# The beginning of a trunk kernel: plain float32 products for the first two weight pieces, and the second k-tile's adaLN weights loaded earlier

## The chip, the cores and the metric

The kernel runs on one core of a Trainium2 chip. TensorE (PE) multiplies, VectorE (DVE) and ScalarE (ACT) do elementwise work, SyncE (SP) issues the loads, and each of them works through its own list of instructions in order. The metric is device microseconds of one execution; less is better. Times inside an execution are counted from the start of the span that the profiler recorded.

## The reference

A decoder trunk with two layers, width 2048, 256 positions, all in float32. The part that matters here is the first layer's input side: a modulation computed from the vector `c`, applied to `x`, and then multiplied with a large weight.

```python
def _adaln(c, w, b):
    mod = jax.nn.silu(c) @ w + b
    shift, scale, gate = jnp.split(mod, 3, axis=-1)
...
h = x * (1.0 + scale) + shift
...
proj = h @ in_w                     # (256, 2048) @ (2048, 10304)
z, xBC, dt = jnp.split(proj, [SSD_D_INNER, SSD_D_INNER + SSD_CONV_DIM], axis=-1)
```

After that come a causal convolution, a chunked state-space scan, an output product, layer norm, shared keys and values, and an attention layer. None of these is touched.

## The kernel before

**h, one k-tile at a time.** The 2048 features of `h` are 16 k-tiles of 128, numbered 0 to 15 here. For each k-tile two 128x2048 arrays of adaLN weights are loaded (`araw`, 1024 KB each, first scale and then shift). DVE multiplies each with silu(c) and sums it along the row (line L279, "a dot" below), then adds the bias (L284, writes `mod`). ACT makes the modulated tile `htmp` out of `xt` and `mod` (L445) and rounds it to a float32r copy, the high part `hhi` (L446); DVE subtracts that from `htmp` and so has the low part `hlo` (L447). Both parts are in the tile that the profile calls `actT`. `xt` is loaded for two k-tiles at once. One call of `h_step` is one dot, and the shift's call also starts the steps behind it.

**Weights, one piece at a time.** A piece is a 128x1024 array (`raw`, 512 KB): two k-tiles by 512 output columns. ACT rounds it to `whi` (L99), DVE makes `wlo` (L101), and PE multiplies three times: whi by hhi, whi by hlo, wlo by hhi. In `cm_piece` (L144 to L146) the weights stand still and 256 positions stream, so that a piece has 24 products, 12 for each k-tile. In `tm_piece` (L198 to L200) `h` stands still and 512 columns stream, with 12 products in a piece. There are 6 buffers for `raw`, 4 for `whi` and 4 for `wlo`; `araw` has 4.

**The order of the beginning.** While `h` is still being made, PE already multiplies those pieces whose k-tiles exist. A table in the program (`order`) lists 58 pieces, 0 to 57. Pieces 0 to 6 need k-tiles 0 and 1 alone, piece 7 is the first that needs k-tiles 2 and 3, and pieces whose accumulation is left off are copied out of PSUM by ACT (`put_away`, L520). Each pass of the loop over `order` fetches a later piece, splits up to two, multiplies one, and calls `h_step` as often as the ratio 4/7 asks. The order in which the instructions then stand on each engine is set by the framework's scheduler when the program is built, by its priorities and by explicit `issue_after` constraints.

**Loads.** All go through SP's list in order. At most eight are outstanding: the ninth waits for the first to land, and so on. A load into a buffer that is still read waits for its reader, and everything behind it on SP's list waits too.

Of the kernel before, what the change touches and what calls it, by code (L numbers as in the profile page):

```python
# [49 lines left out]
def trunk(ctx, tc, xT, x, c, par, cst, bias, lnrow, ada, wdt, win, wxs, wout, wk, wv, wbin, wbout, out):  # L50
# [45 lines left out]
    def split(raw, into=None, after=None):  # L96

        hi, lo = into or [wp.tile([P, 1024], F32R, name=n, bufs=4) for n in ("whi", "wlo")]
        copied.append(S.activation(hi, raw, AF.Copy))  # L99
        with tc.issue_after(after) if after is not None else ExitStack():  # L100
            latest.append(V.tensor_tensor(lo, raw, hi.bitcast(F32), op=ALU.subtract))  # L101
        return hi.rearrange("p (k n) -> p k n", k=2), lo.rearrange("p (k n) -> p k n", k=2)
# [28 lines left out]

    state = [0]

    def cm_piece(src, q, ps, ahi, alo, k0=0, k1=KT, w=None, after=None):


        hi, lo = w or split(load_piece(src[q]), after=after)
        for k in range(2):
            kt = 2 * q + k
            for n in range(4):  # L140
                o = ps[n // 2][:, n % 2, :]
                c_ = slice(n * P, n * P + P)
                first = kt == k0 and n % 2 == 0
                T.matmul(o, hi[:, k, c_], ahi[:, kt, :], start=first, stop=False, skip_group_check=True)  # L144
                T.matmul(o, hi[:, k, c_], alo[:, kt, :], start=False, stop=False, skip_group_check=True)  # L145
                T.matmul(o, lo[:, k, c_], ahi[:, kt, :], start=False, stop=kt == k1 - 1, skip_group_check=True)  # L146

    def acc_pair(pool=None):
        return [(pool or mm).tile([P, 2, L], F32, name="acc") for _ in range(2)]
# [131 lines left out]

    def ada_bias(layer, kts, kinds):
        m = mod[layer][:, kts, kinds]
        V.tensor_tensor(m, m, adab[:, layer, kts, kinds], op=ALU.add)  # L284

    def gate_out(layer):

# [30 lines left out]
    with ExitStack() as cA:  # L318
# [15 lines left out]
        with ExitStack() as cS:  # L334
# [78 lines left out]
            with ExitStack() as c0:  # L413
# [4 lines left out]
                raws, xts, late = [], {}, []  # L418
# [10 lines left out]
                def h_step():  # L429

                    _, kind, kt = cols[h_step.i]
                    raw = raws[h_step.i]
                    h_step.i += 1
                    if kind == "scale" and kt % 2 == 0 and kt:
                        fetch_x(kt)
                    ada_dot(0, kind, kt, raw)
                    if kt > 1:
                        pin[0] = None
                    fetch()
                    while late:  # L440
                        late.pop()()
                    if kind == "shift":
                        ada_bias(0, slice(kt, kt + 1), slice(0, 2))
                        t = pe.tile([P, L], F32, name="htmp")
                        S.activation(t, xts[kt // 2][:, kt % 2, :], AF.Identity, bias=shift(0, kt), scale=scale(0, kt))  # L445
                        S.activation(hhi[:, kt, :], t, AF.Copy)  # L446
# [24 lines left out]
                def fetch_piece():  # L471
                    if len(pieces) < len(order):
                        k, q, _ = order[len(pieces)]
                        pieces.append(load_piece(source[k][q]))

                fetch()
                fetch()
                fetch_x(0)
                nc.sync.dma_start(adab_, par[:, :NB])
                V.tensor_scalar(adab[:, :, :, 1:3], adab[:, :, :, 1:3], 1.0, None, op0=ALU.add)  # L480
                fetch_piece()
                fetch_piece()
                fetch()
                fetch_piece()
                for _ in range(2):
                    for _ in range(2):
                        h_step()
                    while late:
                        pin[0] = late.pop()().ins
                    fetch_piece()  # L490

                def dt_piece(q, raw):

# [25 lines left out]
                            else:  # L519
                                S.activation(place, ps[w], AF.Copy)  # L520

                begin, done, ended, halves = {}, set(), [], {}
                for i, (k, q, ends) in enumerate(order):
                    fetch_piece()
                    if i == 16:
# [677 lines left out]
```

## Time and profile before

| | |
|---|---|
| median of 3 runs | 1247.58 us (1247.24 to 1248.12) |
| the profiled execution | 1247.47 us |
| its span in the profile | 1245.7 us |
| PE busy | 1216.8 us, 98% |
| DVE busy | 1029.4 us, 83% |
| ACT busy | 702.5 us, 56% |
| loads, first five of 40 slices | 381, 422, 421, 422, 421 GB/s |

A slice is 31 us. In the first five slices, which are the part in which `h` is made, the loads run at one constant rate; later they have room. A row of the timeline gives start, duration, engine, line, operation, what is written and read, and, in brackets, how long the engine sat idle before and what released it. A row of the windows gives the stretch, its length and the busy time of each engine, then the clock that PE was granted (1.00 is full), the share of DMA time and the rate.

### The profile page before, as it was taken

The page shows a single profiled execution, that of the slowest core. Times are in us where ns is not written, and L with a number is a line of the kernel's source. Part 1 is how long each engine was busy: PE and PEld are TensorE (multiplying, and loading weights), DVE is VectorE, ACT ScalarE, POOL GpSimd, SP SyncE. Part 2 cuts the span into 40 slices and gives each one's busy share as a digit, 9 for nine tenths or more (in the row PEclk, how much of TensorE's full clock was granted, in tenths as well). Part 3 has the DMA queues.
Part 4 walks back from the last instruction along what each step waited for, and adds up shares of the span by engine and source line. Part 5 has one row for each costly group of instructions (what it writes and reads, how often), then busy time and mean ns, then how long its engine had stood idle before and what let it go on. Part 6 is the DMA issues. An engine that isn't in the chain of part 4 may idle for free.

```text
span 1245.7 us, 18736 instructions
## 1 busy us (share of the span) xinstructions
PE 1216.8 (98%) x7086; PEld 1043.1 (84%) x7086; DVE 1029.4 (83%) x1454; ACT 702.5 (56%) x1045; POOL 0.2 (0%) x4
## 2 busy tenths in 40 slices
PE   4999999999999999999999999999999999999997
PEld 4989998898888888888888788888888888888886
DVE  6999986999987989899768678879888867658777
ACT  3645477868597789654335554443445644445631
POOL 0000000000000000000000000000000000000000
PEclk9999999999999999999999999999999999999999
DMA  9999977687556456699998569988998774463751
GB/s 381 422 421 422 421 266 252 223 287 263 211 186 220 155 183 194 227 334 351 337 333 288 187 213 375 363 329 344 354 382 314 238 242 135 136 204 117 232 175 67
DMA packets 80586, 335.88 MB, mean 270 GB/s; under 512 B 9104, under 2 KB 9328, under 8 KB 67696
## 3 DMA queue, kind: packets, MB, share of 16 engines
q1 hardware_dynamic: 80496, 334.69, 74.6%
q8 instruction: 55, 0.90, 0.3%
q14 instruction: 35, 0.29, 0.1%
HBM read 332.47 MB, written 2.18 MB: 269 GB/s over the span
## 4 chain that ended last, share of the span: by engine, by line
PE 86%; DVE 6%; DMA 4%; ACT 2%; issue 2%; SPq 0%; DVEq 0%; ACTq 0%
PE acc L173 21%; PE acc L199 12%; PE acc L200 12%; PE acc L198 12%; PE acc L176 11%; PE acc L144 3%; PE acc L146 3%; PE acc L145 3%; DMA araw<-in_ada 2%; DVE araw L279 2%; DVE wlo L101 2%; PE py L657 1%; ACT whi L99 1%; PE acc L866 1%; PE aux L969 1%
## 5 line engine op out<-in xcount | busy, mean ns | idle before, releaser
L99 ACT ACTIVATE whi<-raw 128x1024 fp32r<-128x1024 f32 x392 | 411.2, 1058 | 369.9 <-PE acc L200 135.9
L101 DVE TENSOR_TENSOR wlo<-raw,whi 128x1024 fp32r<-128x1024 f32 x392 | 472.7, 1220 | 135.9 <-ACT whi L99 128.5
L173 PE MATMUL acc<-actT,whi 128*128 128x512 f32 x1280 | 405.3, 397 | 0.0
L176 PEld LDWEIGHTS acc<-actT,wlo 128*128 128x128 f32 x1280 | 239.1, 188 | 59.1 <-DVE wlo L101 4.3
L199 PE MATMUL acc<-wlo,actT 128*128 128x512 f32 x656 | 257.5, 393 | 0.6 <-DVE wlo L101 0.5
L176 PE MATMUL acc<-actT,wlo 128*128 128x256 f32 x1280 | 253.4, 279 | 1.7 <-DVE wlo L101 1.2
L198 PE MATMUL acc<-whi,actT 128*128 128x512 f32 x656 | 253.1, 394 | 0.0
L279 DVE SCALAR_TENSOR_TENSOR araw<-araw,cb__72 128x2048 f32<-128x2048 f32 x96 | 219.3, 2285 | 12.1 <-DMA araw<-in_ada 11.8
L173 PEld LDWEIGHTS acc<-actT,whi 128*128 128x128 f32 x1280 | 195.9, 189 | 0.4
L200 PE MATMUL acc<-whi,actT 128*128 128x512 f32 x432 | 168.9, 391 | 0.0
L199 PEld LDWEIGHTS acc<-wlo,actT 128*128 128x128 f32 x656 | 123.2, 188 | 28.0 <-DVE wlo L101 3.1
L198 PEld LDWEIGHTS acc<-whi,actT 128*128 128x128 f32 x656 | 122.5, 188 | 24.2
L144 PE MATMUL acc<-actT,whi 128*128 128x256 f32 x384 | 109.1, 288 | 17.6 <-ACT actT L446 17.4
L145 PE MATMUL acc<-actT,whi 128*128 128x256 f32 x384 | 109.4, 287 | 0.0
L146 PE MATMUL acc<-actT,wlo 128*128 128x256 f32 x384 | 107.5, 287 | 0.9 <-DVE wlo L101 0.9
L200 PEld LDWEIGHTS acc<-whi,actT 128*128 128x128 f32 x432 | 81.1, 188 | 16.6
L144 PEld LDWEIGHTS acc<-actT,whi 128*128 128x128 f32 x384 | 74.5, 195 | 18.6 <-ACT actT L446 17.6
L200 PE MATMUL acc<-whi,ylo 128*128 128x512 f32 x224 | 87.6, 391 | 0.0
L145 PEld LDWEIGHTS acc<-actT,whi 128*128 128x128 f32 x384 | 75.1, 196 | 0.3
L146 PEld LDWEIGHTS acc<-actT,wlo 128*128 128x128 f32 x384 | 73.9, 196 | 1.3 <-DVE wlo L101 1.3
L200 PEld LDWEIGHTS acc<-whi,ylo 128*128 128x128 f32 x224 | 42.1, 188 | 8.5
L615 ACT ACTIVATE seg<-cbc,cumT 128x128 f32<-128x128 f32 x128 | 41.0, 389 | 4.9 <-DVE wlo L101 2.3
(273 smaller groups left out, 1108.8 us busy)
## 6 DMA issues: line engine op xcount, KB each, us to landing
araw<-in_ada SPq DMA_DIRECT2D x96, 1024.0 KB, 7.5
raw<-in_win SPq DMA_DIRECT2D x112, 512.0 KB, 6.8
raw<-in_wout SPq DMA_DIRECT2D x64, 512.0 KB, 5.8
raw<-in_wbin SPq DMA_DIRECT2D x64, 512.0 KB, 3.7
raw<-in_wxs SPq DMA_DIRECT2D x48, 512.0 KB, 4.6
raw<-in_wv SPq DMA_DIRECT2D x48, 512.0 KB, 6.7
raw<-in_wk SPq DMA_DIRECT2D x48, 512.0 KB, 7.1
cbc<-cumd SPq DMA_DIRECT2D x16, 512.0 KB, 4.7
```

Source lines behind the costliest of these rows:

```text
L99: copied.append(S.activation(hi, raw, AF.Copy))
L101: latest.append(V.tensor_tensor(lo, raw, hi.bitcast(F32), op=ALU.subtract))
L144: T.matmul(o, hi[:, k, c_], ahi[:, kt, :], start=first, stop=False, skip_group_check=True)
L145: T.matmul(o, hi[:, k, c_], alo[:, kt, :], start=False, stop=False, skip_group_check=True)
L146: T.matmul(o, lo[:, k, c_], ahi[:, kt, :], start=False, stop=kt == k1 - 1, skip_group_check=True)
L173: T.matmul(ps[n], hi[:, k, n * P:n * P + P], both(kt), start=kt == 0, stop=False, skip_group_check=True)
L176: T.matmul(ps[n][:, 0, :], lo[:, k, n * P:n * P + P], high(kt), start=False, stop=kt == KT - 1, skip_group_check=True)
L198: T.matmul(o, h_, hi[:, k, :], start=kt == k0, stop=False, skip_group_check=part)
L199: T.matmul(o, h_, lo[:, k, :], start=False, stop=False, skip_group_check=part)
L200: end = T.matmul(o, l_, hi[:, k, :], start=False, stop=kt == k1 - 1, skip_group_check=part)
L279: V.scalar_tensor_tensor(raw, raw, 1.0, cb_, op0=ALU.mult, op1=ALU.mult, accum_out=mod[layer][:, ct, j:j + 1])
L615: S.activation(seg[:, hh, b, :], cbc[:, hh, b, :], AF.Relu, bias=cumT[:, b, h0 + hh:h0 + hh + 1], scale=-1.0)
```

## The change

The first two pieces (0 and 1) are no longer split for k-tile 0. Right behind `htmp` of k-tile 0, PE multiplies their raw float32 halves with `htmp` itself, in plain float32: four products for each piece (`plain`) instead of twelve. Only their halves for k-tile 1 are split (`half`, 128x512 arrays), and `cm_piece` is told to do k-tile 1 alone for them (`ks`). Both adaLN arrays of k-tile 1 are loaded ahead of pieces 1 to 4, and two more pieces than before are fetched ahead of the loop. The split of piece 2 is tied behind k-tile 1's high part, and those of pieces 7 and 8 behind the high parts of k-tiles 2 and 3 (`highs`). `ada_bias` returns its instruction so that others can be tied to it.

```diff
-    def cm_piece(src, q, ps, ahi, alo, k0=0, k1=KT, w=None, after=None):
+    def cm_piece(src, q, ps, ahi, alo, k0=0, k1=KT, w=None, after=None, ks=(0, 1)):
         hi, lo = w or split(load_piece(src[q]), after=after)
-        for k in range(2):
+        for k in ks:
...
+                        h_step.bias = ada_bias(0, slice(kt, kt + 1), slice(0, 2))
...
+                        h_step.t, h_step.high = t, S.activation(hhi[:, kt, :], t, AF.Copy)
+                        highs.append(h_step.high.ins)
...
+                def plain(i):
+                    k = order[i][0]
+                    begin[k], pss[k] = 0, acc_pair()
+                    for n in range(4):
+                        T.matmul(pss[k][n // 2][:, n % 2, :], pieces[i][:, n * P:n * P + P], h_step.t,
+                                 start=n % 2 == 0, stop=False, skip_group_check=True)
+
+                def half(i):
+                    halves[i] = [wp.tile([P, 1024], F32R, name=n, bufs=4) for n in ("whi", "wlo")]
+                    hi, lo = (t[:, 512:1024] for t in halves[i])
+                    raw = pieces[i][:, 512:1024]
+                    copied.append(S.activation(hi, raw, AF.Copy))
+                    latest.append(V.tensor_tensor(lo, raw, hi.bitcast(F32), op=ALU.subtract))
+                    halves[i] = [t.rearrange("p (k n) -> p k n", k=2) for t in halves[i]]
...
                 fetch_piece()
-                fetch_piece()
                 fetch()
-                fetch_piece()
-                for _ in range(2):
+                fetch()
+                for _ in range(5):
+                    fetch_piece()
+                for kt in range(2):
                     for _ in range(2):
                         h_step()
+                    if kt == 0:
+                        plain(0)
+                    with tc.issue_after(h_step.bias.ins), tc.issue_after(h_step.high.ins):
+                        half(kt)
                     while late:
                         pin[0] = late.pop()().ins
-                    fetch_piece()
+                    if kt == 0:
+                        plain(1)
+                        fetch_piece()
+                with tc.issue_after(h_step.high.ins), tc.issue_after(pin[0]):
+                    halves[2] = split(pieces[2])
...
-                            halves[j] = split(pieces[j])
+                            with tc.issue_after(highs[j - 5]) if 6 < j < 9 else ExitStack():
+                                halves[j] = split(pieces[j])
...
-                        cm_piece(source[k], q, pss[k], hhi, hlo, k0=k0, k1=k1, w=halves[i])
+                        cm_piece(source[k], q, pss[k], hhi, hlo, k0=k0, k1=k1, w=halves[i], ks=(1,) if i < 2 else (0, 1))
```

What this does to the engines' lists is shown at three places. In the changed kernel the lines behind the new code are 29 higher (L520 is L549, L272 and L93 stay), and hlo's line is L448.

SP's list, from the first two adaLN arrays (k-tile 0) on; `raw` are pieces in their order, `araw` adaLN arrays in theirs, the second `xt` row is that of k-tiles 2 and 3. Before:

```order
L272 DMA araw<-in_ada 128x2048 x2
L427 DMA xt<-in_xT 128x512
L479 DMA adab<-in_par 128x96
L93 DMA raw<-in_win 128x1024 x2
L272 DMA araw<-in_ada 128x2048
L93 DMA raw<-in_win 128x1024
L272 DMA araw<-in_ada 128x2048 x2
L93 DMA raw<-in_win 128x1024
L272 DMA araw<-in_ada 128x2048 x2
L93 DMA raw<-in_win 128x1024 x3
L427 DMA xt<-in_xT 128x512
L272 DMA araw<-in_ada 128x2048
```

SP's list from the same place, in the changed kernel:

```order
L272 DMA araw<-in_ada 128x2048 x2
L427 DMA xt<-in_xT 128x512
L499 DMA adab<-in_par 128x96
L93 DMA raw<-in_win 128x1024
L272 DMA araw<-in_ada 128x2048 x2
L93 DMA raw<-in_win 128x1024 x5
L272 DMA araw<-in_ada 128x2048 x2
L93 DMA raw<-in_win 128x1024
L272 DMA araw<-in_ada 128x2048 x2
L93 DMA raw<-in_win 128x1024 x2
L427 DMA xt<-in_xT 128x512
L272 DMA araw<-in_ada 128x2048
```

K-tile 1's arrays now stand behind one piece instead of two and three; behind them the same loads follow, but the second `xt` stands behind nine pieces and eight arrays instead of seven and seven.

ACT's list from the copy-out of piece 1 (`s_103`) to the split of piece 9; `s_100` is the copy-out of piece 3. Before (the first L99 row is pieces 4 and 5, the next ones 6, 7, and 8 and 9):

```order
L520 ACTIVATE s_103<-acc 128x512 x2
L99 ACTIVATE whi<-raw 128x1024 x2
L520 ACTIVATE s_100<-acc 128x512 x2
L99 ACTIVATE whi<-raw 128x1024
L445 ACTIVATE htmp<-xt,mod_84 128x256
L446 ACTIVATE actT<-htmp 128x256
L99 ACTIVATE whi<-raw 128x1024
L445 ACTIVATE htmp<-xt,mod_84 128x256
L446 ACTIVATE actT<-htmp 128x256
L99 ACTIVATE whi<-raw 128x1024 x2
```

ACT's list at the same place, in the changed kernel (the L99 rows are pieces 5, 6, 7, and 8 and 9):

```order
L549 ACTIVATE s_103<-acc 128x512 x2
L99 ACTIVATE whi<-raw 128x1024
L549 ACTIVATE s_100<-acc 128x512 x2
L99 ACTIVATE whi<-raw 128x1024
L445 ACTIVATE htmp<-xt,mod_84 128x256 x2
L446 ACTIVATE actT<-htmp 128x256
L99 ACTIVATE whi<-raw 128x1024
L446 ACTIVATE actT<-htmp 128x256
L99 ACTIVATE whi<-raw 128x1024 x2
```

Piece 4 moved ahead of the copy-out of piece 1. Both `htmp` (k-tiles 2 and 3) now stand ahead of the first high part, and piece 7's split stands behind them all.

DVE's list from k-tile 1's low part to the split of piece 8, before (the L101 rows are piece 3, then 4 to 6, then 7, then 8; the dots are k-tile 2's first, then its second, then k-tile 3's two):

```order
L447 TENSOR_TENSOR actT<-htmp,actT 128x256
L279 TENSOR_SCALAR araw,mod_84<-araw,cb__72 128x2048
L101 TENSOR_TENSOR wlo<-raw,whi 128x1024
L279 TENSOR_SCALAR araw,mod_84<-araw,cb__72 128x2048
L284 TENSOR_TENSOR mod_84<-mod_84,adab 128x2
L279 TENSOR_SCALAR araw,mod_84<-araw,cb__72 128x2048
L101 TENSOR_TENSOR wlo<-raw,whi 128x1024 x3
L447 TENSOR_TENSOR actT<-htmp,actT 128x256
L279 TENSOR_SCALAR araw,mod_84<-araw,cb__72 128x2048
L284 TENSOR_TENSOR mod_84<-mod_84,adab 128x2
L101 TENSOR_TENSOR wlo<-raw,whi 128x1024
L447 TENSOR_TENSOR actT<-htmp,actT 128x256
```

DVE's list at the same place, in the changed kernel (the L101 rows are pieces 2 to 5, 6, 7 and 8):

```order
L448 TENSOR_TENSOR actT<-htmp,actT 128x256
L493 TENSOR_TENSOR wlo<-raw,whi 128x512
L101 TENSOR_TENSOR wlo<-raw,whi 128x1024 x4
L279 TENSOR_SCALAR araw,mod_84<-araw,cb__72 128x2048 x2
L284 TENSOR_TENSOR mod_84<-mod_84,adab 128x2
L101 TENSOR_TENSOR wlo<-raw,whi 128x1024
L279 TENSOR_SCALAR araw,mod_84<-araw,cb__72 128x2048 x2
L284 TENSOR_TENSOR mod_84<-mod_84,adab 128x2
L448 TENSOR_TENSOR actT<-htmp,actT 128x256
L101 TENSOR_TENSOR wlo<-raw,whi 128x1024
L448 TENSOR_TENSOR actT<-htmp,actT 128x256
L101 TENSOR_TENSOR wlo<-raw,whi 128x1024
```

All four dots of k-tiles 2 and 3 now stand behind the split of piece 5, and the split of piece 7 stands behind k-tile 2's low part. The lists of the two kernels are the same again, line by line, from about 190 us of the profile before to the end.

More of the change, by code (lines that the diff above doesn't have):

```diff
@@ L283, in ada_bias @@
         m = mod[layer][:, kts, kinds]
-        V.tensor_tensor(m, m, adab[:, layer, kts, kinds], op=ALU.add)
+        return V.tensor_tensor(m, m, adab[:, layer, kts, kinds], op=ALU.add)
     def gate_out(layer):
@@ L417, in trunk @@
                 cols = [(0, kind, kt) for kt in range(KT) for kind in ("scale", "shift")]
-                raws, xts, late = [], {}, []
+                raws, xts, late, highs = [], {}, [], []
                 def fetch():
@@ L474, in fetch_piece @@
                         pieces.append(load_piece(source[k][q]))
+                begin, done, ended, halves = {}, set(), [], {}
+                def plain(i):
[11 more added lines that the diff above has]
+                    halves[i] = [t.rearrange("p (k n) -> p k n", k=2) for t in halves[i]]
                 fetch()
@@ L520, in put_away @@
                                 S.activation(place, ps[w], AF.Copy)
-                begin, done, ended, halves = {}, set(), [], {}
                 for i, (k, q, ends) in enumerate(order):
```

2 lines of the change are left out of this document (removed).

## The prediction

> **What bounds the kernel now.** First the page: engines and rates by slices, and the engines' shares of the chain that ended last.
>
> ```profile
> PE   4999999999999999999999999999999999999997
> ...
> GB/s 381 422 421 422 421 266 252 223 287 263 211 186 220 155 183 194 227 334 351 337 333 288 187 213 375 363 329 344 354 382 314 238 242 135 136 204 117 232 175 67
> ...
> PE 86%; DVE 6%; DMA 4%; ACT 2%; issue 2%; SPq 0%; DVEq 0%; ACTq 0%
> ```
>
> PE is the bound but for the first slice, and there the loads run at their top rate. Next the waits of PE alone, 30 to 172 us, then its timeline (the ends of the first three pieces' k-tile 0, the first product with k-tile 1, piece 7's first product and its first with wlo, piece 8's first).
>
> ```profile
> PE acc L146 <- DVE wlo L101: 0.7, 1, 0.7
> ...
> 21.82 0.28 PE L146 MATMUL acc<-actT,wlo 128*128 128x256 f32 x1
> 24.57 0.74 PE L144 MATMUL acc<-actT,whi 128*128 128x256 f32 x4 [2.48 <-ACT actT L446]
> 42.80 0.28 PE L144 MATMUL acc<-actT,whi 128*128 128x256 f32 x1
> 43.27 0.28 PE L146 MATMUL acc<-actT,wlo 128*128 128x256 f32 x1
> 45.67 0.28 PE L144 MATMUL acc<-actT,whi 128*128 128x256 f32 x1
> ```
>
> Pieces 0 to 2 are through with k-tile 0 at 22.1; PE then waits for k-tile 1 until 24.57, and from there to 172 us it waits 0.7 us in all. So a delay of PE in this stretch is a delay of the end, while a head start is worth only what later waits leave of it. I therefore look for the next wait: the chain to k-tiles 1, 2 and 3, from the timelines of ACT and DVE.
>
> ```profile
> 13.01 0.60 ACT L445 ACTIVATE htmp<-xt,mod 128x256 f32<-128x256 f32 x1 [5.79 <-DVE mod L284]
> 18.51 1.06 ACT L99 ACTIVATE whi<-raw 128x1024 fp32r<-128x1024 f32 x1 [2.66 <-DMA raw<-in_win]
> 20.94 2.29 DVE L279 SCALAR_TENSOR_TENSOR araw<-araw,cb__72 128x2048 f32<-128x2048 f32 x1
> 23.28 0.16 DVE L284 TENSOR_TENSOR mod<-mod,adab 128x2 f32<-128x2 f32 x1
> 24.11 0.42 ACT L446 ACTIVATE actT<-htmp 128x256 fp32r<-128x256 f32 x1
> 27.38 1.20 ACT L520 ACTIVATE s<-acc 128x512 f32<-128x512 f32 x2
> 28.66 2.28 DVE L279 SCALAR_TENSOR_TENSOR araw<-araw,cb__72 128x2048 f32<-128x2048 f32 x1
> 31.06 2.28 DVE L279 SCALAR_TENSOR_TENSOR araw<-araw,cb__72 128x2048 f32<-128x2048 f32 x1
> 33.27 3.49 DVE L101 TENSOR_TENSOR wlo<-raw,whi 128x1024 fp32r<-128x1024 f32 x3
> 37.95 2.29 DVE L279 SCALAR_TENSOR_TENSOR araw<-araw,cb__72 128x2048 f32<-128x2048 f32 x1 [0.85 <-DMA araw<-in_ada]
> 39.17 1.06 ACT L99 ACTIVATE whi<-raw 128x1024 fp32r<-128x1024 f32 x1 [3.19 <-DMA raw<-in_win]
> 40.28 0.16 DVE L284 TENSOR_TENSOR mod<-mod,adab 128x2 f32<-128x2 f32 x1
> 40.39 1.23 DVE L101 TENSOR_TENSOR wlo<-raw,whi 128x1024 fp32r<-128x1024 f32 x1
> 40.48 0.60 ACT L445 ACTIVATE htmp<-xt,mod 128x256 f32<-128x256 f32 x1 [0.25 <-DVE mod L284]
> 41.11 0.42 ACT L446 ACTIVATE actT<-htmp 128x256 fp32r<-128x256 f32 x1
> 41.43 1.04 ACT L99 ACTIVATE whi<-raw 128x1024 fp32r<-128x1024 f32 x1
> ```
>
> Piece 7 is split on ACT at 39.17 and on DVE from 40.39 to 41.62, ahead of k-tile 3's htmp (40.48). It is ready 1.65 us before PE takes its wlo (43.27). That is the margin to watch. Last, the price of a plain float32 product, the slow clock's pace, the clock's own stretches, a later piece with little margin (piece 28), and, from the loads of the first 80 us, a piece's time from issue to landing.
>
> ```profile
> 218.98 0.60 PE L602 MATMUL aux<-bcm 128*128 128x256 f32 x2
> 219.42 0.38 PE L603 MATMUL aux<-bcm 128*128 128x128 f32 x2
> ...
> 17.04 0.41 PE L145 MATMUL acc<-actT,whi 128*128 128x256 f32 x1
> 17.26 0.41 PE L146 MATMUL acc<-actT,wlo 128*128 128x256 f32 x1
> ...
> 22.45:25.86 3.41, 1.29 (x10) 1.29 (x11) 2.26 (x5) 1.02 (x2) 0.00 (x0) 1.00 1.02 429
> 25.86:29.27 3.41, 3.41 (x19) 3.41 (x18) 3.08 (x4) 2.85 (x5) 0.00 (x0) 0.51 1.00 422
> 32.70:36.10 3.40, 2.69 (x20) 2.37 (x20) 3.40 (x5) 3.25 (x6) 0.00 (x0) 1.00 1.03 427
> ...
> 99.42 1.23 DVE L101 TENSOR_TENSOR wlo<-raw,whi 128x1024 fp32r<-128x1024 f32 x1
> ...
> 101.72 0.39 PE L199 MATMUL acc<-wlo,actT 128*128 128x512 f32 x1
> ...
> raw<-in_win SPq DMA_DIRECT2D x27, 512.0 KB, 12.2
> ```
>
> **Step 1, the loads.** They land in SP's order at 422 GB/s: 2.49 us for 1024 KB, 1.25 us for 512 KB. Before, a piece, an array and a piece (4.98 us) lie between the first piece's landing and the third's at 18.5, so the first is there at 13.5. What lies ahead of it does not change. In the new order the arrays of k-tile 1 land at 16.0 and 18.5, piece 1 at 19.7, pieces 2 to 5 at 21.0 to 24.7, k-tile 2's arrays at 27.2 and 29.7, piece 6 at 30.9, k-tile 3's at 33.4 and 35.9, pieces 7 and 8 at 37.1 and 38.4, and the xt of k-tiles 2 and 3 at 39.0. Reckoned in the same way from 18.5, the old order's last array of k-tile 3 would land at 36.6; it did at 37.9. So what lands after 36 may be 1.3 later: xt at 39.0 to 40.3.
>
> **Step 2, the head start.** K-tile 0's htmp ends at 13.6; plain products can start then instead of at 14.95. A plain one takes 0.44 warm (218.98 to 219.42, one product in two records). At the slow clock, where a float32r product takes 0.21 instead of 0.12 (20 of them from 43.27 to 45.67), I take twice that, 0.88. Piece 0 takes 3.5, to 17.1. Piece 1 lands at 19.7 and takes 3.3 (nearly all slow), to 23.0. The eight replace 24 products and half of two splits, about 1.2 us of DVE. K-tile 1: dot from 18.5 to 20.8, bias 0.16, htmp 0.60, high part 0.42, so 22.1 instead of 24.53. PE goes on at 23.0 with k-tile 1 of pieces 0 and 1 (24 by 0.12, to 25.9), piece 2 (24, to 28.8), piece 3 (12 by 0.23, to 31.5), pieces 4 to 6 (72, to 40.1). There it was at 42.8: 2.7 us ahead.
>
> **Step 3, where it is lost.** ACT copies out piece 1 after 25.9, behind piece 4's split and piece 0's copy-out: two copies of 0.6 to 27.5, then piece 5's high part to 28.5, DVE's low part to 29.8. Only now come the dots of k-tiles 2 and 3, all four behind it on DVE, 2.40 apart (28.66 to 31.06): two to 34.6, piece 6's low part (a third of 3.49) to 35.8, two more to 40.6, bias to 40.75. Both htmp stand ahead on ACT, so k-tile 2's high part, which could run at 35, waits for k-tile 3's htmp: that to 41.4, high part to 41.85, piece 7's high part to 42.8, its low part to 44.05. If xt lands at 40.3, two htmp of 0.6, overlapping by 0.1, end at 41.4 too. Behind the waiting htmp on ACT stand pieces 7, 8 and 9, and PE for piece 7. PE can begin four products at 42.8 and the first with wlo at 44.05 instead of 43.27: **0.8 us late**, after about 3.5 us of waiting from 40.1 on.
>
> **Step 4, the clock.** A stretch of 3.41 us in which PE was busy for 1.29 us was followed by one at a granted clock of 0.51; one with 2.69 busy was not. The new wait leaves some stretch with 0.5 to 1.4 us busy, so another slow stretch follows. All at work, it costs 3.41 by a half, 1.7 us. Bounds: 0, if no stretch falls so, and 3.4, if release takes two; if the first 1.15 us of it still fall into the wait, 1.1. I take 1.7, what the trace shows for one.
>
> [...]
>
> **Behind piece 7.** The loads land in the same mutual order but for xt, and DVE and ACT have the same number of operations, so a PE that comes later finds more margin. I put the pairing of the high parts in later k-tiles at nothing; cover: the margin that pieces have, 1.65 at piece 7 and 1.07 at piece 28, plus the delay itself; were it gone, each late high part would cost its lateness. SP now waits for piece j's split before it loads piece j+6; cover: the loads ahead of it, since a piece lands 12.2 us after its issue; with that gone, it would cost what the load is late. `ks` and the returned instructions cost nothing, no instruction stands behind them.
>
> **The sum.** 0.8 + 1.7 = 2.5 us on the profiled execution's 1247.47 (span 1245.7 and 1.8 around it; the median is 0.11 higher): **1250.0 us**. Own range of this case: 1248.9 (clock 0.6, since part of the slow stretch falls in the wait) to 1251.7 (clock 3.4).
>
> **Rivals.**
> *The head start survives.* If k-tile 3 were through early enough for piece 7's wlo to be there by 40.5, PE would keep its 2.7 us until the next margin: piece 28's wlo ends at 100.65 and PE takes it at 101.72, so 1.07 is the most that remains, 1246.4 us. For it: k-tile 3's arrays land 2 us earlier than before. Against: DVE, not the landing, holds their dots, by 4.7 us (40.6 against 35.9). It ends faster from the point where wlo of piece 7 is ready before 43.27, 0.8 us earlier than I reckon.
> *The wait comes, the clock stays.* 0.8 alone, 1248.3 us. For it: one stretch with 2.69 busy passed. Against: 1.29 did not.
> *The beginning stays slow.* If the gap between the two plain groups (17.1 to 19.7) keeps the clock low to 25.9, k-tile 1's products of pieces 0 and 1 take 5 us instead of 2.9. Their copy-outs, piece 5's split and the four dots follow, 1.3 us later. 0.8 + 1.3 + 1.7 gives 1251.3 us. It is also what comes if k-tile 1's arrays do not land earlier after all, since then PE passes pieces 0 and 1 later by about as much.
>
> **How the numbers follow.** A measurement of this kernel tells about 0.2%, 2.5 us, from no change, so faster means below 1245.1 and slower above 1250.1. My case 0.50, its own range more above 1250.1 than below (0.30 slower, 0.20 within); clock stays 0.14, within; slow beginning 0.24, slower; head start 0.12, of which 0.03 within at its own price, and 0.09 faster, should the margins behind piece 8 move too. Slower 0.54, within 0.37, faster 0.09. The range leaves out the head start and the slow beginning with two slow stretches: 1247.8 to 1252.2.
>
> **What would show it.** Right: PE's first row at 13.6, a second group at 19.7; k-tile 1's high part near 22; PE waiting near 40 to 44 for whi and wlo of piece 7; DVE's bias of k-tile 3 near 40.7; a granted clock of 0.5 for 3.4 us behind 43; nothing new in PE's waits later. Wrong: no PE wait ahead of piece 7; the four dots earlier than 30; or new waits at pieces beyond 8, which would mean that the pairing of the high parts or SP's longer reach costs what I put at nothing.

## The result, and the profile after

Nineteen executions of each kernel: 1249.72 us median for the changed one (1247.90 to 1252.98), 1248.11 us for the one before (1246.67 to 1249.06). The ratio is 1.0016, 95% interval 1.0009 to 1.0023: slower by 0.16%, about 2 us. The profiled execution took 1249.42 us with a span of 1247.6, against 1247.47 and 1245.7: 1.95 us more.

The page of the changed kernel, rows as they were shown of before:

```profile
PE   4999999999999999999999999999999999999997
...
GB/s 385 421 422 422 421 256 239 223 300 250 214 196 204 169 177 196 219 338 346 346 330 286 191 206 383 345 349 334 356 374 321 239 244 136 136 203 119 229 177 67
...
PE 84%; DMA 6%; DVE 6%; issue 2%; ACT 1%; SPq 0%; DVEq 0%; ACTq 0%
```

Little can be seen at this scale. DMA's share of the chain has gone from 4% to 6%, ACT's from 2% to 1%. The timeline of PE says more: the two plain groups, the first product with k-tile 1, piece 6's last, piece 7's first and its first with wlo, a product behind a wait at 163, and the transposes of `dtrow`, which stand on PE shortly behind the two `dt` pieces, near the end of the table of pieces, and so serve as a mark.

```profile
13.75 3.78 PE L484 MATMUL acc<-htmp,raw 128*128 128x256 f32 x8 [13.75 <-ACT htmp L445]
19.59 3.73 PE L484 MATMUL acc<-htmp,raw 128*128 128x256 f32 x8 [2.06 <-DMA raw<-in_win]
22.82 0.62 PE L144 MATMUL acc<-actT,whi 128*128 128x256 f32 x1
40.16 0.28 PE L146 MATMUL acc<-actT,wlo 128*128 128x256 f32 x1
41.90 0.38 PE L144 MATMUL acc<-actT,whi 128*128 128x256 f32 x1 [1.45 <-ACT whi L99]
43.16 0.38 PE L146 MATMUL acc<-actT,wlo 128*128 128x256 f32 x1 [0.52 <-DVE wlo L101]
163.25 0.39 PE L145 MATMUL acc<-actT,whi 128*128 128x256 f32 x1 [0.41 <-DVE actT L448]
176.34 0.33 PE L538 MATMUL acc<-cc,dtrow 64*128 64x64 f32 x2
```

The same mark before, and from PE's waits up to 235 us one that only the kernel before has (at 221 us):

```profile
174.20 0.33 PE L509 MATMUL acc<-cc,dtrow 64*128 64x64 f32 x2
...
PE aux L626 <- DVE cb L605: 0.3, 1, 0.3
```

At the mark the changed kernel is 2.14 us behind. PE is 2.4 us ahead at 40.44 (piece 6 ends there; piece 7 began at 42.80 before), waits 1.45 and 0.52, and takes piece 7's low part at 43.16, against 43.27 before: level. In this execution the granted clock is on record at 1.00 from 23.14 for 20.480 us, at 0.50 from 43.62 for 3.413 us, then at 1.00 for 1198.078 us: 6, 1 and 351 times 3.413. A stretch of 3.41 us counted from such borders is called a clock period here. What then costs the 2 us is seen in the windows of two of them (columns: busy time of PE, its weight loads, DVE, ACT, POOL, then the granted clock):

```profile
40.20:43.62 3.42, 1.45 (x11) 1.04 (x10) 2.17 (x4) 3.35 (x6) 0.00 (x0) 1.00 1.03 428
43.62:47.03 3.41, 3.41 (x19) 3.41 (x18) 3.41 (x4) 1.45 (x3) 0.00 (x0) 0.50 1.00 414
```

PE was busy for 1.45 of 3.42 us, and the next 3.41 us ran at half clock (a slow stretch): reckoned as half of it, 1.71 us lost. The wait at 163.25 costs another 0.57 (the product stands 0.69 behind its forerunner instead of 0.12). Sum: -0.11 + 1.71 + 0.57 = 2.17, against 2.14 at the mark. The wait of 0.34 us that of these two only the kernel before has, at 221 us, takes that to 1.8, and the spans end 1.9 apart. From 43 us to the mark no other wait of PE differs.

Why piece 7 waits, from ACT and DVE after: piece 5's low part, the first of the four dots, the last, the bias of k-tile 3, and then what stands ahead of piece 7's low part.

```profile
28.20 1.23 DVE L101 TENSOR_TENSOR wlo<-raw,whi 128x1024 fp32r<-128x1024 f32 x1 [1.18 <-ACT whi L99]
29.34 2.29 DVE L279 SCALAR_TENSOR_TENSOR araw<-araw,cb__72 128x2048 f32<-128x2048 f32 x1
37.34 2.29 DVE L279 SCALAR_TENSOR_TENSOR araw<-araw,cb__72 128x2048 f32<-128x2048 f32 x1
39.67 0.16 DVE L284 TENSOR_TENSOR mod<-mod,adab 128x2 f32<-128x2 f32 x1
41.87 1.23 DVE L101 TENSOR_TENSOR wlo<-raw,whi 128x1024 fp32r<-128x1024 f32 x1 [0.52 <-ACT whi L99]
...
39.49 1.10 ACT L445 ACTIVATE htmp<-xt,mod 128x256 f32<-128x256 f32 x2 [6.10 <-DMA xt<-in_xT]
40.50 0.40 ACT L446 ACTIVATE actT<-htmp 128x256 fp32r<-128x256 f32 x1
40.80 1.04 ACT L99 ACTIVATE whi<-raw 128x1024 fp32r<-128x1024 f32 x1
```

ACT waited 6.10 us for xt, then made both htmp, a high part, and only then piece 7's whi. So piece 7's low part ends 3.3 us behind the bias (43.10 against 39.83); before it ended 1.2 behind (41.62 against 40.44).

### The profile page after: what moved, and what is told of

It is laid out like the page before. It is cut to its first block, busy times and chain, and to the rows that moved or that the text cites. A ratio compares the mean times of both kernels' runs of the same rounds, so it can differ in the third digit from the quotient of the medians.

```text
span 1247.6 us, 18723 instructions
## 1 busy us (share of the span) xinstructions
PE 1219.1 (98%) x7078; PEld 1043.9 (84%) x7078; DVE 1028.5 (82%) x1454; ACT 701.0 (56%) x1045; POOL 0.2 (0%) x4
## 4 chain that ended last, share of the span: by engine, by line
PE 84%; DMA 6%; DVE 6%; issue 2%; ACT 1%; SPq 0%; DVEq 0%; ACTq 0%
PE acc L173 20%; PE acc L199 12%; PE acc L200 12%; PE acc L198 12%; PE acc L176 10%; PE acc L146 3%; PE acc L144 3%; PE acc L145 3%; DMA raw<-in_wk 2%; DVE araw L279 2%; DMA araw<-in_ada 2%; DVE wlo L101 1%; PE py L686 1%; DMA xt<-in_xT 1%; DMA raw<-in_wv 1%
## 5 line engine op out<-in xcount | busy, mean ns | idle before, releaser
L99 ACT ACTIVATE whi<-raw 128x1024 fp32r<-128x1024 f32 x390 | 409.4, 1058 | 352.8 <-PE acc L200 137.6
L101 DVE TENSOR_TENSOR wlo<-raw,whi 128x1024 fp32r<-128x1024 f32 x390 | 469.7, 1222 | 134.0 <-ACT whi L99 129.8
L173 PEld LDWEIGHTS acc<-actT,whi 128*128 128x128 f32 x1280 | 195.9, 189 | 0.4
L144 PE MATMUL acc<-actT,whi 128*128 128x256 f32 x376 | 107.0, 287 | 1.5 <-ACT whi L99 1.5
L145 PE MATMUL acc<-actT,whi 128*128 128x256 f32 x376 | 106.5, 285 | 0.4 <-DVE actT L448 0.4
L144 PEld LDWEIGHTS acc<-actT,whi 128*128 128x128 f32 x376 | 72.9, 194 | 2.3 <-ACT whi L99 1.7
L145 PEld LDWEIGHTS acc<-actT,whi 128*128 128x128 f32 x376 | 72.8, 194 | 1.0 <-DVE actT L448 0.6
```

The lines of the kernel that those rows point to most:

```text
L173: T.matmul(ps[n], hi[:, k, n * P:n * P + P], both(kt), start=kt == 0, stop=False, skip_group_check=True)
```

## The experiments

The theory: piece 7's wait, which comes from ACT's chain behind the late xt, eats the head start, and the half clock behind the wait makes the loss. Rivals: the loads alone hold piece 7; the plain products or the order of k-tile 1's arrays cost the time; the clock has nothing to do with the wait.

**xt earlier.**

```diff
                 for _ in range(5):
                     fetch_piece()
+                fetch_x(2)
...
-                    if kind == "scale" and kt % 2 == 0 and kt:
+                    if kind == "scale" and kt % 2 == 0 and kt > 2:
                         fetch_x(kt)
```

> The changed kernel with one load moved: the xt of k-tiles 2 and 3 is issued ahead of k-tile 2's arrays instead of behind piece 8, so that it lands near 26 us instead of 39.4. Theory of the wait at piece 7: k-tile 2's htmp no longer waits 6.1 us for xt, the high parts of k-tiles 2 and 3 no longer stand behind it, piece 7's low part is written from 39.8 to 41.1 and PE takes it at 41.1 to 41.3 instead of 43.16; the wait shrinks from 1.97 to 0.5-0.9 us, no slow stretch follows it, and the time goes from 1249.4 to about 1247.5 (1246.4 to 1248.4: what is won beyond 1 us is lost again at pieces 9 to 11, whose loads land no earlier). Rival, the loads alone hold piece 7: PE's wait stays near 2 us and the time at 1249.4. Rival, the products in plain float32 cost the time: the time stays at 1249.4 though the wait has gone.

Measured: 1247.43 us median, ratio to before 0.9994 (0.9985 to 1.0003); the changed kernel's interval lies wholly above 1. PE's one wait at piece 7, and DVE there:

```profile
41.67 0.39 PE L146 MATMUL acc<-actT,wlo 128*128 128x256 f32 x1 [0.66 <-DVE wlo L101]
...
40.28 0.16 DVE L284 TENSOR_TENSOR mod<-mod,adab 128x2 f32<-128x2 f32 x1
40.39 1.22 DVE L101 TENSOR_TENSOR wlo<-raw,whi 128x1024 fp32r<-128x1024 f32 x1
```

The bias is even 0.6 later than in the changed kernel, but piece 7's low part follows at once, and no slow stretch follows the wait. Moving one load of 256 KB gives back what the change had cost. It does so through ACT's order, which the scheduler sets anew, and not by the landing alone. In the changed kernel xt landed at 39.41 and the bias ended at 39.83, so with both htmp still ahead of the first high part an earlier xt could have saved only about 0.1 us (an estimate from these two times and ACT's rows). Here piece 7's whi is made at 39.15, ahead of k-tile 3's htmp at 40.48. PE takes the low part at 41.67, later than the 41.1 to 41.3 expected, because the bias came later. Both rivals named there fall: the loads did not hold piece 7, and the plain products were still in it.

**Separate the two htmp.**

```diff
-                        S.activation(t, xts[kt // 2][:, kt % 2, :], AF.Identity, ...)
+                        with tc.issue_after(highs[-1]) if highs else ExitStack():
+                            S.activation(t, xts[kt // 2][:, kt % 2, :], AF.Identity, ...)
```

> The changed kernel with each k-tile's htmp held on ACT until the high part of the k-tile before it has been made, so that two htmp never stand ahead of both high parts. Theory: the wait of 0.41 us for k-tile 15's low part at 163.25 us goes (0.57 us in PE's rows), and piece 7's low part comes about 0.4 earlier (42.75 instead of 43.16): 1248.4 to 1248.9. Rival, the pairing costs nothing, as I had put it: 1249.4 and the same lag of 2.1 us against before at 172 us.

Measured: 1249.56, 1.0012 (1.0004 to 1.0021), no better than the changed kernel. The wait for k-tile 15's low part only fell to 0.29. So the order of the high parts on ACT is not its cause; my expectation missed. Piece 7's low part was taken at 42.85, near the 42.75 expected; so with xt still landing at 39.45 the order alone gains 0.3 us there. A new wait of 0.55 stands at piece 8.

**Drop the rule on pieces 7 and 8.**

```diff
-                            with tc.issue_after(highs[j - 5]) if 6 < j < 9 else ExitStack():
-                                halves[j] = split(pieces[j])
+                            halves[j] = split(pieces[j])
```

> The changed kernel without the rule that pieces 7 and 8 are split only behind the high parts of k-tiles 2 and 3. Theory of the wait at piece 7: xt still lands at 39.4, so k-tile 2's high part still comes near 41; both low parts of the pieces now stand ahead of k-tile 2's low part on DVE, which moves from 41.36 to about 42.6. PE waits as long as before or longer (1.5 to 2.2 us), one slow stretch follows: 1248.9 to 1249.9. Rival, the rule itself makes the wait: the wait falls under 0.7 us and the time to 1247.5.

Measured: 1249.17, 1.0005 (0.9996 to 1.0014). PE waited 1.45 us for k-tile 2's high part and 0.2 for its low part: the wait stays, it only has another name. But no slow stretch followed: the clock period that took in the wait, 40.78 to 44.19, was busy for 2.05 us. That part of the expectation was wrong, and it says something on the clock (below).

**Fill the wait.**

```diff
+                zero = pe.tile([P, P], F32R, name="zero", bufs=1)
+                S.activation(zero, ones, AF.Copy, scale=0.0)
...
+                        for _ in range(10 if i == 7 else 0):
+                            T.matmul(pss[k][0][:, 0, :], zero, hhi[:, 0, :], start=False, stop=False, ...)
                         cm_piece(source[k], q, pss[k], hhi, hlo, ...)
```

> The changed kernel with ten further products of 128x256 ahead of piece 7's, with a weight tile of zeros and k-tile 0 as data, added to piece 7's accumulator, which they leave as it is; they can run in the wait from 40.44 to 41.9 and take 1.2 us there at full clock. Nothing comes earlier by them. Theory of the clock: PE is busy for 2.6 instead of 1.4 of the 3.41 us, the granted clock stays at 1.0 from 43.6 to 47.0, and the time falls by 1.7 to about 1247.7, with fewer executions above 1250. Rival, the clock costs nothing or the slow stretch does not come from this wait: 1249.4, or up to 1.2 more if the ten products delay piece 7.

Measured: 1248.94, 1.0007 (0.9999 to 1.0016). In the profiled execution the clock periods lie as they did in the changed kernel's (to 0.05 us), and piece 7's low part is taken at 43.16 in both, so they can be compared directly:

```profile
40.16:43.57 3.41, 2.67 (x20) 2.27 (x19) 2.12 (x4) 3.41 (x6) 0.00 (x0) 1.00 1.03 425
43.57:46.98 3.41, 3.41 (x31) 3.41 (x30) 3.41 (x4) 2.39 (x4) 0.00 (x0) 1.00 1.00 417
...
174.84 0.33 PE L540 MATMUL acc<-cc,dtrow 64*128 64x64 f32 x2
```

Ten products that nobody needs bring the mark forward by 1.50 us (174.84 against 176.34), and the granted clock behind them is 1.00 instead of 0.50. So the half clock does come from the wait, and it costs about what the theory says (1.71). The median did not fall to the 1247.7 expected: by the ratios, 1.0007 against 1.0016, the gain over all executions is about 1.1 us, and the two intervals overlap. That not every execution has its periods there would explain the difference; only one execution was profiled, so this is not shown.

**The changed kernel once more.**

> The changed kernel once more, for another execution's profile and for times beside those of the kernels sent with it. [...] The times of the executions spread over 1247.7 to 1251. [...]

Measured: 1249.75, 1.0018 (1.0010 to 1.0027). The profiled execution again had a wait of 1.46 and 0.52 us, a period with 1.43 busy (40.23 to 43.64), and the slow stretch behind it (43.64 to 47.05, against 43.62 to 47.03 in the first execution); the mark stands at 176.48. With the stretch in the same place, this run does not tell whether it belongs to the program. In other kernels with the same beginning the granted clock was 0.50 elsewhere: from 20.66 to 24.07 with xt early, from 20.30 to 23.71 without the rule on pieces 7 and 8. And of the two executions of the version with xt early and k-tile 15's low part ahead, one had it at 0.50 from 20.70 to 24.12, while the other's mean over the whole span was 1.000. So one program can run with such a stretch and without.

**The loads without the plain products; the plain products with k-tile 1's second array behind piece 1.**

```diff
-                    if kt == 0:
-                        plain(0)
...
-                        half(kt)
+                        halves[kt] = split(pieces[kt])
...
                     if kt == 0:
-                        plain(1)
                         fetch_piece()
...
-                        cm_piece(source[k], q, pss[k], hhi, hlo, k0=k0, k1=k1, w=halves[i], ks=(1,) if i < 2 else (0, 1))
+                        cm_piece(source[k], q, pss[k], hhi, hlo, k0=k0, k1=k1, w=halves[i])
```

> The changed kernel with its new order of loads and its new prefetch, but without the plain float32 products: pieces 0 and 1 are split whole and multiplied in three products each, as before. Theory of the wait at piece 7: PE starts near 15 and passes piece 6 about 1 us later than with plain products (41 to 41.5 instead of 40.4), waits less there, and takes piece 7's low part at 43.2 all the same; so the time is that of the changed kernel, or lower where the shorter wait brings no slow stretch: 1247.7 to 1249.4. The plain products then are worth nothing to the end. Rival, plain products save time that lasts: 1250.5 or more. Rival, plain products cost time: 1247.5, and piece 7's low part is taken before 42.5.

```diff
                 fetch()
-                fetch()
-                for _ in range(5):
+                fetch_piece()
+                fetch()
+                for _ in range(4):
                     fetch_piece()
```

> The changed kernel with one load moved back: the second array of k-tile 1 again comes behind piece 1, as the pieces and arrays alternated before, and the plain products and the deeper prefetch stay. Theory of the wait at piece 7: k-tile 1's high part comes 1.2 us later (23.2 instead of 21.9), PE passes piece 6 up to 1 us later, xt still lands at 39.4 and piece 7's low part is taken at 43.1 to 43.3; the time is 1247.7 to 1249.4. Rival, the order of k-tile 1's arrays is what makes the difference to before: piece 7's low part moves by about 1.2 us and the time with it, to 1248.2 or to 1250.6.

Measured: 1250.41, 1.0022 (1.0013 to 1.0031), and 1249.55, 1.0013 (1.0005 to 1.0022), beside 1.0018 for the changed kernel on the same chip: all three overlap. I had expected piece 7's low part at 43.2 in both; it was taken at 44.74 and 44.48, with no slow stretch behind it. In both the bias of k-tile 3 came late (41.54, 41.28), because PE was slow in the beginning instead: in the first the 18 products from 22.75 to 26.16 took 0.19 us each, in the second a slow stretch fell here:

```profile
20.39:23.80 3.41, 0.45 (x2) 0.30 (x2) 2.22 (x4) 1.51 (x4) 0.00 (x0) 1.00 1.03 423
23.80:27.22 3.42, 3.42 (x17) 3.41 (x17) 3.05 (x3) 3.42 (x6) 0.00 (x0) 0.50 1.02 429
```

A slow stretch at 24 to 27 delays pieces 0 and 1, their copies, piece 5's split and the dots, and is paid at piece 7; one at 44 to 47 is paid behind piece 7. A loss of the same size stands there without the plain products too, so they are not needed for it; beyond that the two runs do not tell which part of the change costs more.

**xt earlier, and k-tile 15's low part ahead of the next piece's.**

```diff
                     while late and h_step.i % 4 == 0:
-                        late.pop()()
+                        low = late.pop()()
+                        if h_step.i == len(cols):
+                            pin[0] = low.ins
...
-  ... if 6 < j < 9 else ExitStack():
+  ... if 6 < j < 9 else tc.issue_after(pin[0]) if pin[0] is not None else ExitStack():
```

> The changed kernel with xt of k-tiles 2 and 3 loaded early, as in xt_early, and with the low part of the next piece held on DVE until the low part of k-tile 15 has been made. Theory: the wait ahead of piece 7 stays at 0.5 to 0.9, and PE's wait of 0.69 us for k-tile 15's low part near 160 goes, since that part comes 1.1 us earlier; 0.4 to 0.7 below xt_early, 1246.8 to 1247.1, and below the kernel before. Rival, the order on DVE only moves the wait to the next piece's low part: as xt_early, 1247.4.

> The version with xt early and the low part of k-tile 15 ahead, once more, for times beside those of the two sent with it. Expected 1246.5 (1246.0 to 1247.0), with a ratio to before below 1 again; the wait ahead of piece 7 0.4 to 0.7 us and none near 160.

Measured: 1246.51, 0.9989 (0.9980 to 0.9998), and again 1246.15, 0.9993 (0.9983 to 1.0003). First DVE near 160 with xt early alone, then in this version:

```profile
157.73 0.16 DVE L284 TENSOR_TENSOR mod<-mod,adab 128x2 f32<-128x2 f32 x1
157.81 2.36 DVE L101 TENSOR_TENSOR wlo<-raw,whi 128x1024 fp32r<-128x1024 f32 x2
160.09 0.75 DVE L448 TENSOR_TENSOR actT<-htmp,actT 128x256 fp32r<-128x256 f32 x2
```

```profile
158.34 0.16 DVE L284 TENSOR_TENSOR mod<-mod,adab 128x2 f32<-128x2 f32 x1
158.41 1.23 DVE L101 TENSOR_TENSOR wlo<-raw,whi 128x1024 fp32r<-128x1024 f32 x1
159.56 0.75 DVE L448 TENSOR_TENSOR actT<-htmp,actT 128x256 fp32r<-128x256 f32 x2
```

The kernel before, in which PE does not wait there either, has one piece's low part ahead as well, and the changed kernel has two:

```profile
158.35 1.23 DVE L101 TENSOR_TENSOR wlo<-raw,whi 128x1024 fp32r<-128x1024 f32 x1
159.56 0.43 DVE L447 TENSOR_TENSOR actT<-htmp,actT 128x256 fp32r<-128x256 f32 x1
...
160.50 2.36 DVE L101 TENSOR_TENSOR wlo<-raw,whi 128x1024 fp32r<-128x1024 f32 x2
162.78 0.76 DVE L448 TENSOR_TENSOR actT<-htmp,actT 128x256 fp32r<-128x256 f32 x2
```

With two pieces' low parts ahead of those of k-tiles 14 and 15 and xt early, PE waited 0.69 us; with one ahead it does not wait there in either execution of this version. So that wait came from DVE's order. This version beats the changed kernel, and the kernel before by 0.1% in the first of its two measurements; the second interval reaches just past 1.

**Warm the clock ahead.**

```diff
+                def warm(n):
+
+                    for _ in range(n):
+                        T.matmul(first[0][0][:, 0, :], zero[:, :P], zero, start=True, stop=True, ...)
...
+                warm(76)
                 fetch()
                 fetch()
...
-                        plain(0)
+                        with tc.issue_after(plain(0).ins):
+                            warm(24)
```

> The changed kernel with 76 products of a tile of zeros ahead of the first plain group and 24 between the two plain groups, whose sums nothing reads; they keep PE at work from about 2 to 13 us and from 15.7 to 18.6. Theory: the granted clock is at 1.0 when the first plain product starts, so each plain group takes 1.9 instead of 3.7 us, and PE ends piece 6 one to two us earlier than 40.4. But the wait for piece 7 hangs on the high parts of k-tiles 2 and 3 behind xt and on DVE's dots, which come no more than 1 us earlier; PE only waits longer (2.5 to 3.5 us), and a slow stretch follows: 1248.4 to 1249.4, no gain worth more than 1 us. Rival, the slow beginning is the loss: with it gone the time falls under 1247.5.

> The same products of zeros in the version with xt early and with the low part of k-tile 15 ahead of the next piece's. Theory: there piece 7's low part stands right behind DVE's fourth dot, which hangs on PE through the copies out of piece 1 and through piece 5's split; a full clock from the start brings the dots forward by up to 1 us, until the landing of k-tile 3's second array (36.3 to 37.9) holds them. 0.5 to 1 us below xt_low: 1245.5 to 1246.3. Rival, the loads hold it already: 1246.5 as xt_low.

Measured: 1252.00, 1.0031 (1.0020 to 1.0042), and 1248.18, 1.0001 (0.9992 to 1.0009): no gain, against both expectations. The intervals touch those without the warming (1.0010 to 1.0027; 0.9983 to 1.0003), so a loss is not shown either. The first plain group did take 1.89 us instead of 3.78. But k-tile 1's second array landed at 19.83 and 19.72 instead of 18.31, and with it everything behind k-tile 1 came late: piece 7's low part was taken at 45.69 and 43.20. In the first, slow products behind the wait for piece 1 came on top: the second plain group took 3.41 us from 21.11, and only from 24.95 on did the products stand 0.12 apart. What made the array late is not shown. So these two say nothing on a warm beginning by itself.

**The best version without the plain products.**

> The version with xt early and the low part of k-tile 15 ahead, without the plain float32 products: pieces 0 and 1 are split whole and take three products each. Theory: there the bias of k-tile 3 is all that piece 7 waits for, and it hangs on DVE's dots behind piece 5's split, which comes later by the two half splits (1.2 us of DVE) and by PE's later passage of pieces 0 and 1; the bias comes at 41.5 to 42 instead of 40.5 to 41.3, piece 7's low part is taken near 43, and the time is 1246.8 to 1247.8, that is, the plain products are worth 0.5 to 1.3 us there. Rival, they are worth nothing: 1246.2 to 1246.5, with the bias at 40.5 to 41.3 too.

Measured: 1248.46, 1.0001 (0.9992 to 1.0010), against 0.9989 and 0.9993 with them; by these ratios the plain products are worth 1.0 to 1.5 us. The bias of k-tile 3 ended at 42.36 instead of 41.33 and 40.51, piece 7's low part was taken at 43.59, and the mark stands at 174.62, 1.0 and 1.9 us later than with them. The direction is that of the theory; but the intervals overlap, and the bias was at its latest in an execution that was slow at its beginning (30 products in 7.23 us of PE's work from 15 to 26 us, 0.24 each). Probably the plain products are worth something once piece 7 no longer stands behind ACT's chain; these runs don't prove it.

**One sum for all executions.** From piece 7's low part to the mark the kernel before needs 130.93 us. Add 1.71 for a slow stretch behind piece 7 and what the wait for k-tile 15's low part costs:

| execution | low part taken | slow behind | k-tile 15 | sum | mark |
|---|---|---|---|---|---|
| before | 43.27 | | | | 174.20 |
| changed | 43.16 | 1.71 | 0.57 | 176.37 | 176.34 |
| changed, again | 43.29 | 1.71 | 0.57 | 176.50 | 176.48 |
| filled wait | 43.16 | | 0.57 | 174.66 | 174.84 |
| loads only | 44.74 | | 0.57 | 176.24 | 176.43 |
| array behind piece 1 | 44.48 | | 0.57 | 175.98 | 176.19 |
| xt early | 41.67 | | 0.85 | 173.45 | 173.64 |
| xt early, low part ahead | 42.56 | | | 173.49 | 173.59 |
| the same, again | 41.74 | | | 172.67 | 172.76 |
| the same, no plain products | 43.59 | | | 174.52 | 174.62 |
| warmed | 45.69 | 1.71 | 0.57 | 178.90 | 178.75 |
| warmed, xt early | 43.20 | | | 174.13 | 174.21 |

All agree within about 0.2 us. (Without the rule on pieces 7 and 8 the first product with wlo, at 42.86, comes one product earlier in PE's list; with 0.12 for that one and 0.57 for k-tile 15 the sum is 174.48, the mark 174.55. With the two htmp apart the sum is 0.5 short, even with the waits at piece 8 and k-tile 15 in it; that stayed open.) So three things set the time of this stage: when piece 7's low part is there, whether the wait for it brings half clock, and the wait near 160.

The mark is not the end. Between it and the end of the span, where nothing was changed, the distance to the kernel before moves from one execution to the next: by 1.1 us down with the two htmp apart (1.18 behind at the mark, 0.1 at the end), by 1.3 us up without the rule on pieces 7 and 8 (0.35 and 1.7). What moves it was not looked for. It is as large as most differences between the kernels here, so the sum accounts for this stage, and one execution's time says little on a single step.

The two executions of the same best kernel show the part of chance: slow products up to 25.87 (16 in the 3.41 us before it, 0.21 each), bias 41.33, mark 173.59, against a slow stretch from 20.70 to 24.12, spent while PE was ahead anyway, 40.51 and 172.76. Between these two executions this kernel differs by 0.8 us at the mark.

## Why the prediction was right, and where it was not

The time, 1250.0 in 1247.8 to 1252.2, was borne out: 1249.72. More than half of the chance had gone to slower by over 0.2%, and the ratio says 0.16%, so the sign was right and the size at the edge of what I called measurable.

- *Step 1, the loads.* Right to 0.3 us up to k-tile 3's first array: k-tile 1 at 15.80 and 18.31 (16.0, 18.5), piece 1 at 19.55 (19.7), k-tile 2 at 26.95 and 29.40 (27.2, 29.7); k-tile 3's second array 0.4 late at 36.34; xt at 39.41, inside 39.0 to 40.3.
- *Step 2, the head start.* Right: 13.75, 19.59, k-tile 1 from 22.82, piece 6's end 40.44 for 40.1, so 2.4 us ahead instead of 2.7. A plain group took 3.78 and 3.73, not 3.5 and 3.3: four products in 3.78 are 0.94 each at the slow clock.
- *Step 3, where it is lost.* The place and the chain were right: both htmp ahead of the high part, then whi and wlo of piece 7. The term was mis-sized: 0.8 late, measured -0.1. The dots began at 29.34 instead of 29.8: two copies of 0.6 from 25.9 end at 27.1, and I had gone on from 27.5. They stood 2.2 apart, not 2.40 (between the two rows that I took it from lies a gap of 0.12), so the bias came at 39.8 instead of 40.75. PE waited 2.0, not 3.5. I had put xt's lateness beside the bias as a second bound; in the run the two came within 0.4 us of each other, so that neither alone held the chain, and the first experiment shows what I had not seen: with xt in time the scheduler also puts piece 7's split ahead of k-tile 3's htmp, and the whole chain behind the bias falls away.
- *Step 4, the clock.* Right in size and place, 43.62 to 47.03 at 0.50 in the profiled execution; the filled wait puts its price at 1.50 for the 1.7 reckoned. Gaps of 1.45 and 0.52 us with 0.7 us of products between them stood ahead of it.
- *Behind piece 7, "nothing".* Wrong by 0.57 us, and I had named the sign of it: new waits beyond piece 8. My suspect there, the pairing of the high parts, is not the cause; with the pairing undone 0.29 of 0.41 us of the wait remained. The cause is DVE's order, where the next piece's low part stands ahead of both k-tiles' low parts. "The same number of operations" was no cover: order, not count, decided.
- *The rivals.* "The beginning stays slow" looks less like a rival to my case than like its other face: in the execution with the array behind piece 1, PE was slow from 24 to 27 and piece 7 came late, and in the two profiled executions of the changed kernel it was slow behind piece 7. At the mark the cost is nearly the same (176.19 and 176.34). Whether the changed kernel itself has both kinds of execution was not seen. "The clock stays" did not happen in either profiled execution of the changed kernel; the filled wait shows what it would have been worth.
- The errors had opposite signs: -0.9 in step 3, +0.6 behind piece 7, -0.3 for a wait of the kernel before that fell away. That they nearly cancel is luck: the sum was better than its terms. The forecast difference was 2.5 us; measured are 1.95 between the profiled executions and 1.6 between the medians. The median of the kernel before lies 0.6 above the 1247.47 that the sum started from, which also helped the time.

## What to carry to other kernels

A head start lasts only to the next thing that the same engine waits for; follow that one's chain through every engine's order before counting the gain, and look there for a small load that the new prefetch has pushed back: here 256 KB loaded 14 us earlier took the whole loss back. When steps are paired or moved, read the order on each engine, since counts of operations hide one step that now stands behind another. Look at the clock behind a short wait too: here waits of 1.45 and 0.52 us were followed by 3.41 us at a granted clock of 0.50, and ten products put into the wait brought the mark forward by 1.50 us.

## What the runs showed of the hardware

- The stretches of granted clock on record last 6.827, 3.413 and 1215.145 us in the kernel before, from 19.07 on, and 20.480, 3.413 and 1198.078 us in the changed one, from 23.14 on: 2, 1 and 356, and 6, 1 and 351 times 3.413. In each the one of 3.413 is at half clock, the others are at full; from 1244.46 and 1245.11 to the end of the span the clock is at half again.
- Half clock came after a period with this much PE work: 0.45 us (the array behind piece 1, 20.39 to 23.80), 0.92 (without the rule on pieces 7 and 8, 16.88 to 20.30), 1.08 (xt early and low part ahead, again, 17.29 to 20.70), 1.12 (xt early, 17.24 to 20.66), 1.33 (before, 22.48 to 25.90), 1.43 (changed, again) and 1.45 (changed). The clock stayed full after 2.05 (without the rule on pieces 7 and 8, 40.78 to 44.19), 2.26 and 2.32 (the array behind piece 1, 16.98 to 20.39 and 40.87 to 44.28) and 2.67 (the filled wait, 40.16 to 43.57). Whether the work alone decides is not shown.
- In the beginning the products stayed slow after periods with 2.56 us of work (changed, 12.90 to 16.31), 2.63 (the two htmp apart, 14.85 to 18.26) and 2.80 (xt early and low part ahead, 19.05 to 22.46); full clock came after 3.26 (before, 15.66 to 19.07) and 3.42 (changed, 19.72 to 23.14). The clock column shows 1.00 until the first recorded change, so there the slow clock is seen only in the products (before, 0.21 from 16.83 to 17.04 instead of 0.12) and not in the column, nor in an execution's mean.
- K-tile 3's second array landed late in both kernels: before, 4.01 us behind the load ahead of it (33.92 to 37.92), in the changed one 3.18 (33.16 to 36.34), where the other arrays of 1024 KB from 13 to 33 us took 2.41 to 2.51. The queue that the page lists as "instruction" (q8) moved its first packet of 16 KB while that array was on its way, at 35.75 and 33.56. That the one made the other late is not shown: when the same queue moved its next packet in the kernel before, at 51.22, the array on its way took 2.50, and no run moved one alone.
